# A softmax step queued behind the next head's shuffle, and weight halves made at other points, in a float32 transformer kernel on one core

## The chip, the cores and the metric

The kernel runs on one core of a Trainium2 chip. The metric is the device time of one execution in microseconds (us). TensorE is called PE below, VectorE DVE, ScalarE ACT, GpSimd POOL, and SyncE, which issues most DMAs, SP.

## The reference

Two blocks are computed for 256 tokens of width 1024 in float32. The first is two layers: a differential attention with 8 heads (this is where the main edit lies), a feed-forward, a short gated convolution, a feed-forward, each with a layer norm. The second is a parallel mixer, a cross attention to 256 memory tokens, and a product-key expert layer with 16384 experts, each with an RMS norm in front. Of the differential attention:

```
q, k: rotated on their first 16 of 64 dims; two score maps per head (c = 0, 1)
p = softmax(mask(q k / 8))                    # per map
a = p[0] - lam * p[1]
o = rms_norm(a @ v, g_sub) * (1 - lam_init)
out = o @ w_o
```

## The kernel before

**Weights.** Every product is made of three matmuls with a high and a low part of each operand (`mm3`, L329 to L331). `Stream` loads the weights in units of 1 MB by SP into two `raw` buffers, in the order of use. A unit has two halves. `pre(n)` makes the high parts of all halves below n on ACT (L231, tile `wh`); `split(n)` makes the low parts (L243, tile `wl`, `raw - wh`) on the engine that `W.sub` names for the half: V is DVE, G is POOL. When both halves of a unit are split, its `raw` buffer is free and the next load is issued. Order is manual: every engine runs its instructions in the order in which the program emits them.

**Attention.** A loop over 13 steps `st` is a pipeline over the 8 heads h. In step st: PE projects q and k of head st (`qk_proj`, ACT copies them out, L660), transposes the weights `at` of head st-3 (`pv_a`) and the output of head st-5 (`o_T`, low part on DVE, L749), multiplies by v for head st-4 (`pv_b`; ACT squares, L732; DVE rs2a, L325; POOL the inverse root, L320). `qk_rot` rotates head st: a shuffle on DVE (L666), then three products and sums on POOL (L668, L670, L672), which PE's scores wait for. `scores` of head st-1: PE (L683), DVE the maxima (L685 to L687), ACT the exponentials (L689, L696). `pv_n` scales on DVE (L739). `W.split` makes two low halves on DVE for the head after next. `soft` (L703 to L708) turns the exponentials of a head into `at`: six DVE instructions, a reciprocal, a product with lambda, and twice a scaling and a fused product and sum. From step 8 on there is no rotation, and PE multiplies by `wo0` and projects memory keys (`mem_k0`, `mem_k1`) between the heads.

**Boundaries.** `finish` ends a layer: last matmuls for token halves t = 0 and 1 (`last_mm`), residual and norm (`fa`, `fb`), transposes on PE (`to_T`), with a piece of memory projection (`mem_v`, `mem_k`) on PE as cover. `finish_two` is the one in front of the mixer, where a layer norm and an RMS norm follow each other; the one with `early=2` is the mixer's output boundary. `lam` makes lambda from 256 numbers.

Of the kernel before, what the change touches and what calls it, by code (L numbers as in the profile page):

```python
# [263 lines left out]
def body(ctx, tc, I, O):  # L264
    nc = tc.nc
    V, A, P, G = nc.vector, nc.scalar, nc.tensor, nc.gpsimd
# [136 lines left out]
    LNS = {}  # L403
# [36 lines left out]
    def rms_b(src, key, gb):  # L440
        ss = LNS.pop(key)
        a = sm([128, 2], name="ssa")
        V.tensor_scalar(a[:, 0:1], ss[:, 0:1], 1.0 / D, 1e-6, op0=OP.mult, op1=OP.add)
        V.scalar_tensor_tensor(a[:, 1:2], ss[:, 1:2], 1.0 / D, a[:, 0:1], op0=OP.mult, op1=OP.add)
        rs = inv_sqrt_pool(a[:, 1:2], 1, "rs1")
        if "hg" in LNS:
            r = LNS.pop("hg")
            V.tensor_scalar(r[:, 0:512], r[:, 0:512], rs, None, op0=OP.mult)
            A.activation(r[:, 512:], r[:, 512:], AF.Copy, scale=rs)
            return r  # L450
        r = wp.tile([128, D], F32, name="r")
        for s in (slice(0, 512), slice(512, 1024)):
            V.scalar_tensor_tensor(r[:, s], src[:, s], rs, gb[:, s], op0=OP.mult, op1=OP.mult)
        return r
# [10 lines left out]
    def last_mm(acc, items, t, nb, part=None):  # L465
        n = len(items)
        a, b = (0, n) if part is None else (0, n // 2) if part == 0 else (n // 2, n)
        for i in range(a, b):
            x, kt, w, j = items[i]
            wj = w(j)  # L470
            c = nb * 512
            mm3(acc[t][nb], x[0][:, kt, t * 128:t * 128 + 128], x[1][:, kt, t * 128:t * 128 + 128],
                wj[0][:, c:c + 512], wj[1][:, c:c + 512], False, i == n - 1)

    def finish_two(acc, items, fa, fb, x, fa0, fb0):
        last_mm(acc, items, 1, 0)
        last_mm(acc, items, 1, 1)
        W.sub = [V, V]
        W.pre(2 * W.i + 3)
        r0 = fb(0)  # L480
        fa(1, 0)
        fa(1, 1)
        W.split(2 * W.i + 3)
        W.sub = [G, G]
        W.look = 0
        for g in fa0:
            g()
        r1 = fb(1)
        W.split(2 * W.i + 2)
        src0 = r0()  # L490
        src1 = r1()
        for g in fb0:
            g()
        T0 = to_T(src0, 0, x, True)
        T0()
        W.split(2 * W.i + 1)
        to_T(src1, 1, x)
        W.split(2 * W.i + 2)
        W.look = 2
        W.sub = [V, V]  # L500
# [5 lines left out]
    def finish_any(acc, items, fa, fb, x, fa0=(), fb0=(), two=False, early=0, first=2, warm=0):  # L506
        if fb0 and not two:
            W.sub = [V, G]
        for nb in range(2):
            last_mm(acc, items, 0, nb, 0)  # L510
        for nb in range(2):
            last_mm(acc, items, 0, nb, 1)
            if nb == 0:
                W.sub = [G, G]
                W.split(2 * W.i + first)
            fa(0, nb)
        if two:
            return finish_two(acc, items, fa, fb, x, fa0, fb0)
        src0 = fb(0)
        last_mm(acc, items, 1, 0)  # L520
        if early:
            W.sub = [V, V]
            last_mm(acc, items, 1, 1)
            W.pre(2 * W.i + first + early)
        if early == 2:
            W.split(2 * W.i + first + 1)
        fa(1, 0)
        if early == 2:
            W.split(2 * W.i + first + 2)
        if not early:  # L530
            last_mm(acc, items, 1, 1)
        fa(1, 1)
        if callable(src0):
            src0 = src0()
        W.look = 0
        for f in fa0:
            f()
        W.look = 2
        T0 = to_T(src0, 0, x, True)
        if warm:  # L540
            ps = bank()
            xf = items[0][0][0].rearrange("p a b -> p (a b)")
            for i in range(warm):
                P.matmul(ps, xf[:, 0:128], xf[:, 0:512], start=True, stop=True)
        src1 = fb(1)
        if callable(src1):
            src1 = src1()
        T0()
        if early != 1:
            W.split(2 * W.i + 2)  # L550
        for f in fb0:
            f()
        to_T(src1, 1, x)
        W.sub = [V, V]
# [77 lines left out]
    for nb in range(2):  # L632
        pss = [bank(), bank()]
        for hf in range(2):
            w = W.get(("v0", nb * 2 + hf))
            proj_mov(pss, w, xT, hf * 4)
            if (nb, hf) == (1, 0):
                mem_norm(0)
                lam()
        for t in range(2):  # L640
            A.activation(v0[:, t, nb * 512:nb * 512 + 512], pss[t], AF.Copy)

# [8 lines left out]
    def abank(name, ok):  # L651
        return accp.tile([128, 512], F32, name=name) if ok else bank()
# [88 lines left out]

    def o_T(h):
        on = ON.pop(h)
        ps = abank("acc01", h < 3)
        for t in range(2):
            ts = slice(t * 128, t * 128 + 128)
            P.transpose(ps[:, ts], on[:, ts], ident)
        A.activation(oT[0][:, h, :], ps[:, :256], AF.Copy, scale=gs)
        V.scalar_tensor_tensor(oT[1][:, h, :], ps[:, :256], gs, oT[0][:, h, :].bitcast(F32), op0=OP.mult,  # L749
                               op1=OP.subtract)  # L750
# [38 lines left out]
    for st in range(8 + 5):  # L789
        W.look = 0 if 0 < st < 9 else 2  # L790
        if st < 8:
            qk_proj(st)
        if st in (1, 2):
            low = to_T(mem_in[st - 1], st - 1, mT, True)
        if st == 8:
            acc = acc_banks()
        if st in (8, 9):
            w_o(acc, oT, "wo0", st - 8)
        if st == 10:
            mem_k0(0)  # L800
        if st == 11:
            mem_k1(0)
        if st == 12:
            w_o(acc, oT, "wo0", 2, js=(0,))
        if 0 <= st - 3 < 8:
            pv_a(st - 3)
        if 0 <= st - 5 < 8:
            o_T(st - 5)
        if st == 12:
            w_o(acc, oT, "wo0", 2, js=(1,))  # L810
            W.split(2 * W.i + 4)
        if 0 <= st - 4 < 8:
            pv_b(st - 4)
        if st < 8:
            qk_rot(st)
        if st in (1, 2):
            low()
        if st == 0:
            W.split(2 * W.i + 3)
        if 0 <= st - 1 < 8:  # L820
            W.pre(2 * W.i + 4)
            if st == 1:
                W.split(2 * W.i + 2)
            scores(st - 1)
            if 0 <= st - 4 < 8:
                pv_n(st - 4)
            W.split(2 * W.i + 4)
        elif 0 <= st - 4 < 8:
            pv_n(st - 4)
        if 0 <= st - 1 < 8:  # L830
            soft(st - 1)

    def ln_boundary(acc, items, h, gi, fa0, fb0, early=0):
        hn = hp.tile([128, 2, D], F32, name="h")
# [895 lines left out]
```

## Time and profile before

| | |
|---|---|
| median of 3 runs | 1673.63 us (1673.27 to 1678.7) |
| the profiled execution | 1675.48 us |
| its span, first to last instruction | 1673.2 us |
| mean granted PE clock | 0.997 of full speed |
| busy: PE, DVE, ACT, POOL | 1642.3, 1168.1, 818.4, 442.5 us |

Times in the rows are us from the span's start. The profiled execution's own time is 2.3 us more than its span and 1.85 us more than the median. A busy time is an average over stages that are bounded by different engines, so it has to be read stage by stage.

### The profile page before, as it was taken

How to read it: one execution, taken by the hardware profiler on the slowest of the kernel's cores; microseconds unless marked ns; L12 is line 12 of the kernel's file. 1: busy time of each engine (PE TensorE's matmuls, PEld its weight loads, DVE VectorE, ACT ScalarE, POOL GpSimd, SP SyncE). 2: the span in 40 equal slices, each digit the busy share in tenths (PEclk: the TensorE clock that was granted, in tenths of full speed). 3: DMA queues.
4: the chain of work that ended last, by engine and by line, in shares of the span. 5: the costliest groups of instructions: out<-in, count | busy, mean ns of one | idle time of the engine just before them, and what ended most of it. 6: DMA issues, size and time to landing. Idle time of an engine off the chain costs nothing.

```text
span 1673.2 us, 27599 instructions
## 1 busy us (share of the span) xinstructions
PE 1642.3 (98%) x11024; PEld 1496.0 (89%) x11024; DVE 1168.1 (70%) x2076; ACT 818.4 (49%) x1268; POOL 442.5 (26%) x434
## 2 busy tenths in 40 slices
PE   8999999999999998999999999999999999999997
PEld 7989999899999986987989999999999888888886
DVE  5987554666655456776458898889898666666665
ACT  5664444444444445765454555444443544444444
POOL 0532000110300002001015788788611211111111
PEclk9999999999999999999999999999999999999999
DMA  8446777555555563534355666666544656566664
GB/s 286 154 144 238 246 243 239 176 202 200 199 194 178 201 227 138 179 104 168 112 195 152 191 188 180 192 184 181 149 151 140 213 202 222 203 220 203 219 203 176
DMA packets 80416, 317.48 MB, mean 190 GB/s; under 512 B 25120, under 2 KB 41760, under 8 KB 45344
## 3 DMA queue, kind: packets, MB, share of 16 engines
q1 hardware_dynamic: 59120, 304.38, 53.0%
q0 software_dynamic: 20736, 10.56, 4.2%
q8 instruction: 86, 1.41, 0.3%
q10 hardware_dynamic: 432, 0.79, 0.1%
q14 instruction: 42, 0.34, 0.1%
HBM read 303.04 MB, written 10.55 MB: 187 GB/s over the span
## 4 chain that ended last, share of the span: by engine, by line
PE 57%; DVE 2%; ACT 1%; DMA 1%; issue 1%; POOL 0%; POOLq 0%; ACTq 0%; SPq 0%; DVEq 0%
PE mm L329 10%; PE mm L331 10%; PE mm L330 10%; PE acc L330 8%; PE acc L329 7%; PE acc L331 7%; PE acc L1600 2%; DVE wl L243 1%; DMA big<-in_subk_dram 0%; PE mm L1479 0%; PE mm L1355 0%; PE mm L1322 0%; DMA raw<-in_ws_dram 0%; DMA raw<-in_vec_dram 0%; POOL rs L320 0%
## 5 line engine op out<-in xcount | busy, mean ns | idle before, releaser
L243 DVE TENSOR_TENSOR wl<-raw,wh 128x1024 fp32r<-128x1024 f32 (+1 forms) x525 | 644.8, 1247 | 249.8 <-ACT wh L231 248.6
L231 ACT ACTIVATE wh<-raw 128x1024 fp32r<-128x1024 f32 (+1 forms) x537 | 553.8, 1055 | 375.7 <-PE acc L331 180.0
L329 PE MATMUL mm<-xTh,wh 128*128 128x256 f32 x2328 | 659.5, 283 | 0.0
L331 PE MATMUL mm<-xTh,wl 128*128 128x256 f32 x2328 | 654.9, 281 | 2.0 <-DVE wl L243 2.0
L330 PE MATMUL mm<-xTl,wh 128*128 128x256 f32 x2328 | 654.3, 281 | 0.0
L329 PEld LDWEIGHTS mm<-xTh,wh 128*128 128x128 f32 x2328 | 440.8, 189 | 3.8 <-issue 1.0
L331 PEld LDWEIGHTS mm<-xTh,wl 128*128 128x128 f32 x2328 | 440.6, 189 | 3.1 <-DVE wl L243 3.1
L330 PEld LDWEIGHTS mm<-xTl,wh 128*128 128x128 f32 x2328 | 440.8, 189 | 0.8
L1511 POOL DMA_INDIRECT gd<-slots,idx x128 | 252.3, 1971 | 84.7 <-issue 32.0
L330 PE MATMUL acc<-wl,xTh 128*128 128x512 f32 x632 | 251.4, 398 | 0.6 <-DVE wl L243 0.6
L329 PE MATMUL acc<-wh,xTh 128*128 128x512 f32 x632 | 250.1, 396 | 1.7 <-DVE xTl L749 1.4
L331 PE MATMUL acc<-wh,xTh 128*128 128x512 f32 x504 | 197.6, 392 | 0.0
L329 PEld LDWEIGHTS acc<-wh,xTh 128*128 128x128 f32 x632 | 118.6, 188 | 32.3 <-DVE xTl L749 1.9
L330 PEld LDWEIGHTS acc<-wl,xTh 128*128 128x128 f32 x632 | 118.7, 188 | 28.5 <-DVE wl L243 1.9
L1558 POOL TENSOR_TENSOR big<-big,oj 128x256 f32<-128x256 f32 x64 | 57.6, 899 | 289.1 <-DMA oj<-gd 289.1
L243 POOL TENSOR_TENSOR wl<-raw,wh 128x1024 fp32r<-128x1024 f32 x12 | 29.0, 2425 | 324.7 <-ACT wh L231 324.7
L331 PEld LDWEIGHTS acc<-wh,xTh 128*128 128x128 f32 x504 | 94.6, 188 | 22.6
L895 DVE TENSOR_TENSOR sil<-sil,mm 128x256 f32<-128x256 f32 x44 | 18.5, 421 | 104.0 <-ACT sil L894 104.0
L894 ACT ACTIVATE sil<-mm 128x256 f32<-128x256 f32 x44 | 16.9, 385 | 148.6 <-PE mm L331 148.6
L362 DVE TENSOR_TENSOR xTh<-big,xTh 128x256 fp32r<-128x256 f32 x126 | 83.2, 660 | 0.0
L1510 POOL MEMSET spacer<- 1x1 f32 x128 | 78.5, 613 | 0.0
L330 PE MATMUL acc<-wl,hTh 128*128 128x512 f32 x176 | 69.6, 395 | 0.0
(391 smaller groups left out, 1814.1 us busy)
## 6 DMA issues: line engine op xcount, KB each, us to landing
raw<-in_ws_dram SPq DMA_DIRECT2D x131, 1024.0 KB, 5.1
raw<-in_us_dram SPq DMA_DIRECT2D x64, 1024.0 KB, 4.9
raw<-in_vs_dram SPq DMA_DIRECT2D x64, 1024.0 KB, 4.9
gd<-zt SPq DMA_DIRECT2D x32, 256.0 KB, 6.5
raw<-in_pq_dram SPq DMA_DIRECT2D x8, 1024.0 KB, 4.8
oj<-gd SPq DMA_DIRECT2D x64, 128.0 KB, 4.8
gb<-in_vec_dram POOLq DMA_DIRECT2D x12, 512.0 KB
gd<-slots,idx POOLq DMA_INDIRECT x128
```

Source lines behind the costliest of these rows:

```text
L231: self.nc.scalar.activation(h[:, s], self.R[i][:, k * HW:(k + 1) * HW][:, s], AF.Copy)
L243: self.sub[k].tensor_tensor(l[:, s], self.R[i][:, k * HW:(k + 1) * HW][:, s], h.bitcast(F32)[:, s], op=OP.subtract)
L329: P.matmul(ps, lh, rh, start=first, stop=False)
L330: P.matmul(ps, lh, rl, start=False, stop=False)
L331: P.matmul(ps, ll, rh, start=False, stop=last)
L362: V.tensor_tensor(l, src, h.bitcast(F32), op=OP.subtract)
L894: A.activation(s, pg[:, :256], AF.Silu)
L895: V.tensor_tensor(s, s, pg[:, 256:], op=OP.mult)
L1510: G.memset(spacer, 0.0)
L1511: d = G.indirect_dma_start(out=gd, out_offset=bass.IndirectOffsetOnAxis(ap=idx[:, h, k:k + 1], axis=0), in_=gate[:, 0, h, k:k + 1], in_off ...
L1558: G.tensor_tensor(b, b, GT.pop(c), op=OP.mult)
L1600: P.matmul(ps[:, i * 128:i * 128 + 128], oi[:, i, :], oj[:, i, :], start=True, stop=True)
```

## The change

- In the attention loop `soft(st - 1)` at a step's end becomes `soft(st - 2)` right behind `qk_rot(st)`: each head's softmax is emitted one step later, behind the next shuffle and ahead of the maxima.
- `lam()` moves from the value projection into step 0 of that loop.
- `o_T` of head 2 takes a rotating PSUM bank in place of the accumulator bank acc01.
- In front of the mixer, the third half of the two `mem_v` units is split on POOL ahead of the norm's work and the fourth on DVE; before, the third was on DVE behind the norm's first part and the fourth on POOL.
- At the mixer's output boundary, two low halves move from between the norm's instructions to behind them. `rms_b` gets a condition that this order needs.

```diff
@@ rms_b
-        if "hg" in LNS:
+        if key[1] == 1 and "hg" in LNS:
@@ finish_two
-        W.sub = [V, V]
-        W.pre(2 * W.i + 3)
+        W.sub = [G, V]
+        W.split(2 * W.i + 3)
+        W.pre(2 * W.i + 4)
         r0 = fb(0)
         fa(1, 0)
         fa(1, 1)
-        W.split(2 * W.i + 3)
+        W.split(2 * W.i + 4)
@@ finish_any
-        src0 = fb(0)
         last_mm(acc, items, 1, 0)
         if early:
             W.sub = [V, V]
             last_mm(acc, items, 1, 1)
+        if early == 2:
+            fa(1, 0)
+        src0 = fb(0)
+        if early:
             W.pre(2 * W.i + first + early)
-        if early == 2:
-            W.split(2 * W.i + first + 1)
-        fa(1, 0)
-        if early == 2:
-            W.split(2 * W.i + first + 2)
+        if early != 2:
+            fa(1, 0)
...
+        if early:
+            W.split(2 * W.i + 1)
         T0()
-        if early != 1:
+        if not early:
             W.split(2 * W.i + 2)
@@ the value projection
                 mem_norm(0)
-                lam()
@@ o_T
-        ps = abank("acc01", h < 3)
+        ps = abank("acc01", h < 2)
@@ the attention loop
             qk_rot(st)
+        if 0 <= st - 2 < 8:
+            soft(st - 2)
...
             W.split(2 * W.i + 3)
+            lam()
...
-        if 0 <= st - 1 < 8:
-            soft(st - 1)
```

In the attention loop, DVE's queue of one step before, from the two low weight halves of a step through the softmax to the next step's first maxima (`acc_953` is a score bank):

```order
L243 TENSOR_TENSOR wl<-raw,wh 128x1024 x2
L703 RECIPROCAL rc<-su 128x4
L704 TENSOR_TENSOR rc<-rc,nlam 128x2
L707 TENSOR_SCALAR pe<-pe,rc 128x128
L708 SCALAR_TENSOR_TENSOR at<-pe,rc 128x128
L707 TENSOR_SCALAR pe<-pe,rc 128x256
L708 SCALAR_TENSOR_TENSOR at<-pe,rc 128x256
L749 SCALAR_TENSOR_TENSOR xTl_339<-acc_924,gs,xTh_338 128x256
L325 TENSOR_SCALAR rs2a<-oss 128x2
L666 STREAM_SHUFFLE qksw<-qkraw 128x512
L685 MEMSET acc_953 64x2x64
```

The same stretch of the changed kernel, whose lines from the attention on are 2 higher (L705 to L710 are the softmax, L668 is the shuffle):

```order
L243 TENSOR_TENSOR wl<-raw,wh 128x1024 x2
L751 SCALAR_TENSOR_TENSOR xTl_328<-acc_917,gs,xTh_327 128x256
L325 TENSOR_SCALAR rs2a<-oss 128x2
L668 STREAM_SHUFFLE qksw<-qkraw 128x512
L705 RECIPROCAL rc<-su 128x4
L706 TENSOR_TENSOR rc<-rc,nlam 128x2
L709 TENSOR_SCALAR pe<-pe,rc 128x128
L710 SCALAR_TENSOR_TENSOR at<-pe,rc 128x128
L709 TENSOR_SCALAR pe<-pe,rc 128x256
L710 SCALAR_TENSOR_TENSOR at<-pe,rc 128x256
L687 MEMSET acc_953 64x2x64
```

The softmax moved from ahead of the low part of `o_T`, rs2a and the shuffle to directly behind the shuffle; POOL's three rotation instructions, whose queue is unchanged, start when the shuffle ends.

In front of the mixer, POOL's queue before, from the copy of the memory's transposed tile (L978) on; `rs_6578` is the norm of t = 0, `rs_6623` that of t = 1:

```order
L978 DMA xTl_6504<-mTl 128x2048
L320 TENSOR_TENSOR rs_6578<-rs1a,nhalf 128x1
L426 TENSOR_TENSOR h<-r,gb 128x512 x2
L320 TENSOR_TENSOR rs_6623<-rs1a,nhalf 128x1
L243 TENSOR_TENSOR wl<-raw,wh 128x1024
```

And in the changed kernel:

```order
L981 DMA xTl_6504<-mTl 128x2048
L243 TENSOR_TENSOR wl<-raw,wh 128x1024
L320 TENSOR_TENSOR rs_6582<-rs1a,nhalf 128x1
L426 TENSOR_TENSOR h<-r,gb 128x512 x2
L320 TENSOR_TENSOR rs_6629<-rs1a,nhalf 128x1
```

POOL's weight half now stands ahead of the norm's inverse root instead of behind both.

At the mixer's output boundary, DVE's queue before (`acc_7877` and `acc_7878` are the accumulators of t = 0, `acc_7879` and `acc_7880` those of t = 1):

```order
L453 SCALAR_TENSOR_TENSOR r<-h,rs_8129,gb 128x512 x2
L243 TENSOR_TENSOR wl<-raw,wh 128x1024
L458 TENSOR_TENSOR h<-h,acc_7879 128x512
L463 TENSOR_TENSOR r<-h,gb 128x512
L243 TENSOR_TENSOR wl<-raw,wh 128x1024
L458 TENSOR_TENSOR h<-h,acc_7880 128x512
L463 TENSOR_TENSOR r<-h,gb 128x512
```

And in the changed kernel, where the residual of t = 1 begins ahead of the norm of t = 0:

```order
L458 TENSOR_TENSOR h<-h,acc_7879 128x512
L463 TENSOR_TENSOR r<-h,gb 128x512
L443 TENSOR_SCALAR ssa<-ssh 128x1
L444 SCALAR_TENSOR_TENSOR ssa<-ssh,ssa 128x1
L453 SCALAR_TENSOR_TENSOR r<-h,rs_8158,gb 128x512 x2
L458 TENSOR_TENSOR h<-h,acc_7880 128x512
L463 TENSOR_TENSOR r<-h,gb 128x512
L443 TENSOR_SCALAR ssa<-ssh 128x1
L444 SCALAR_TENSOR_TENSOR ssa<-ssh,ssa 128x1
L448 TENSOR_SCALAR r<-r,rs_8213 128x512
L243 TENSOR_TENSOR wl<-raw,wh 128x1024
```

The two halves no longer stand between the residual of t = 0 and that of t = 1; one follows the norm, the other the transposes' low parts.

## Rows read from the trace of the kernel before

**Rows 1.** The first part of the page: busy time, share of the span and instructions of each engine.

```profile
PE 1642.3 (98%) x11024; PEld 1496.0 (89%) x11024; DVE 1168.1 (70%) x2076; ACT 818.4 (49%) x1268; POOL 442.5 (26%) x434
```

**Rows 2.** Busy time of the engines (PE, PE's weight loads, DVE, ACT, POOL, each with its instructions) in two stretches of 20 us of the attention; the last three columns are PE's granted clock, DMA share and GB/s.

```profile
60.00:80.00 20.00, 18.92 (x157) 17.66 (x155) 19.39 (x46) 12.83 (x38) 10.19 (x8) 1.00 0.51 176
80.00:100.00 20.00, 17.10 (x128) 15.12 (x128) 19.42 (x49) 11.33 (x37) 13.03 (x11) 1.00 0.40 141
```

**Rows 3.** What PE waited for between 34 and 142 us: us in total, times, longest.

```profile
PE acc L683 <- POOL qk L672: 1.8, 3, 0.8
PE acc L329 <- DVE xTl L749: 1.4, 1, 1.4
...
PE mm L683 <- POOL qk L672: 0.7, 1, 0.7
```

**Rows 4.** The attention in order of time, DVE: shuffles of heads 2, 5, 6 and 7, and between those of 5 and 6 the instructions with which the parts of a step begin (three of the softmax); last, a pair of low halves with POOL idle. Start, duration, engine, line, operation.

```profile
53.74 0.76 DVE L666 STREAM_SHUFFLE qksw<-qkraw 128x512 f32<-128x512 f32 x1
...
79.67 0.75 DVE L666 STREAM_SHUFFLE qksw<-qkraw 128x512 f32<-128x512 f32 x1
80.43 0.17 DVE L685 MEMSET acc<- 64x128 f32 x1
82.52 3.82 DVE L243 TENSOR_TENSOR wl<-raw,wh 128x1024 fp32r<-128x1024 f32 x2
86.27 0.16 DVE L703 RECIPROCAL rc<-su 128x4 f32<-128x4 f32 x1
86.46 0.16 DVE L704 TENSOR_TENSOR rc<-rc,nlam 128x2 f32<-128x2 f32 x1
86.98 0.35 DVE L708 SCALAR_TENSOR_TENSOR at<-pe,rc 128x128 f32<-128x128 f32 x1
88.04 0.48 DVE L749 SCALAR_TENSOR_TENSOR xTl<-acc,gs,xTh 128x256 fp32r<-128x256 f32 x1
88.50 0.73 DVE L666 STREAM_SHUFFLE qksw<-qkraw 128x512 f32<-128x512 f32 x1
...
97.32 0.73 DVE L666 STREAM_SHUFFLE qksw<-qkraw 128x512 f32<-128x512 f32 x1
...
108.35 2.35 DVE L243 TENSOR_TENSOR wl<-raw,wh 128x1024 fp32r<-128x1024 f32 x2
```

**Rows 5.** The attention in order of time, POOL: the rotation of head 0, and that of head 5.

```profile
39.18 1.29 POOL L668 TENSOR_TENSOR qksw<-qksw,rope 128x512 f32<-128x512 f32 x1 [4.84 <-DVE qksw L666]
40.43 2.28 POOL L670 TENSOR_TENSOR qk<-qkraw,rope 128x512 f32<-128x512 f32 x1
...
80.50 1.29 POOL L668 TENSOR_TENSOR qksw<-qksw,rope 128x512 f32<-128x512 f32 x1
81.76 1.30 POOL L670 TENSOR_TENSOR qk<-qkraw,rope 128x512 f32<-128x512 f32 x1
83.13 2.13 POOL L672 TENSOR_TENSOR qk<-qk,qksw 128x512 f32<-128x512 f32 x1
```

**Rows 6.** DVE and POOL at once, elsewhere, in order of time: a weight half on DVE during the rotation of head 0; the norm's fused products on DVE during POOL's weight half in front of the mixer; a small DVE instruction during POOL's products L1137 in the mixer.

```profile
39.28 2.27 DVE L243 TENSOR_TENSOR wl<-raw,wh 128x1024 fp32r<-128x1024 f32 x1 [0.18 <-ACT wh L231]
...
632.30 2.50 POOL L243 TENSOR_TENSOR wl<-raw,wh 128x1024 fp32r<-128x1024 f32 x1
632.49 3.53 DVE L428 SCALAR_TENSOR_TENSOR h<-r,rs,gb 128x512 f32<-128x512 f32 x2
...
737.72 2.52 POOL L1137 TENSOR_TENSOR h<-h,gb 128x512 f32<-128x512 f32 x2 [52.97 <-ACT r L1136]
739.29 0.98 DVE L1139 TENSOR_SCALAR ss<-ss 128x8 f32<-128x8 f32 x1
```

**Rows 7.** The same attention step, ACT: the scaling of the maxima, with which the exponentials begin, and the end of the squares behind them.

```profile
82.12 0.21 ACT L689 ACTIVATE nb<-mx 128x4 f32<-128x4 f32 x1 [3.25 <-DVE mx L687]
...
85.57 0.26 ACT L732 ACTIVATION_READ_ACCUMULATOR on<-acc 128x1 f32 x1
```

**Rows 8.** PE in the attention: the scores of step 5, and the first matmul of step 11.

```profile
85.31 0.93 PE L683 MATMUL acc<-qk 64*128 64x128 f32 x8 [0.75 <-POOL qk L672]
...
115.43 0.36 PE L329 MATMUL mm<-mTh,wh 128*128 128x256 f32 x1
```

**Rows 9.** The value projection: PE's wait behind lambda.

```profile
31.88 0.39 PE L331 MATMUL mm<-xTh,wl 128*128 128x256 f32 x1 [0.76 <-DVE wl L243]
```

**Rows 10.** In front of the mixer: the high part of the third half on ACT; PE's two waits for low halves, and its first transposes.

```profile
622.18 1.06 ACT L231 ACTIVATE wh<-raw 128x1024 fp32r<-128x1024 f32 x1 [1.26 <-DMA raw<-in_ws_dram]
...
631.00 0.50 PE L330 MATMUL mm<-wl,mTh 128*128 128x512 f32 x1 [2.43 <-DVE wl L243]
634.86 0.50 PE L330 MATMUL mm<-wl,mTh 128*128 128x512 f32 x1 [0.79 <-POOL wl L243]
637.82 1.32 PE L370 MATMUL mm<-cst,r 128*128 128x128 f32 x8
```

**Rows 11.** The mixer's output boundary: two low halves on DVE, PE's two waits in the transposes.

```profile
785.93 1.22 DVE L243 TENSOR_TENSOR wl<-raw,wh 128x1024 fp32r<-128x1024 f32 x1
788.39 1.22 DVE L243 TENSOR_TENSOR wl<-raw,wh 128x1024 fp32r<-128x1024 f32 x1
...
792.56 0.63 PE L370 MATMUL mm<-cst,r 128*128 128x128 f32 x4 [2.46 <-ACT xTh L373]
793.63 1.11 PE L370 MATMUL mm<-cst,r 128*128 128x128 f32 x4 [0.44 <-ACT r L449]
```

## The prediction

> **What bounds the kernel now.** The busy times come first: PE works 98% of the span [rows 1], so about 31 us is all that can be won, and only a stretch in which PE stands idle can give any of it. The stretches of the attention come next: between 60 and 100 us PE lacks 1.08 and 2.90 us, while DVE is busy 19.4 of 20 us in both [rows 2]. That is the sign of another bound: in these steps DVE sets the pace and PE waits. What PE waits for there is the rotated head (L672 on POOL, 1.8 and 0.7 us) and the release of an accumulator bank (1.4 us) [rows 3].
>
> So I read DVE's queue in order of time. From the shuffle of head 5 to that of head 6 it takes 8.83 us without a gap [rows 4]: shuffle 0.76, maxima and the scaling behind them 2.09 (80.43 to 82.52), two low halves 3.75, softmax 1.77 (86.27 to 88.04), the low part of `o_T` with rs2a 0.46. PE's own work in a step is this less its wait of 0.75 [rows 8], 8.1 us. The low halves take 3.82 here and 2.35 at 108.35, where POOL is idle [rows 4]: 1.47 us of the step is lost while POOL rotates.
>
> **How DVE and POOL lock each other.** The rotation of head 0 shows it. A low half is issued 0.10 us after L668 and takes 2.27 us [rows 6] where half a pair takes 1.2: it stands until L668 ends (40.45) and then runs 1.1, to 41.55. L670, next on POOL, takes 2.28 instead of 1.30: it stands until the low half ends and then runs [rows 5]. So one instruction at a time goes through, and the two engines take turns. The softmax's own kinds are held too: two fused products took 3.53 us, to 636.02, since POOL's half ran to 634.80, and a TENSOR_SCALAR on 128x8, however small, took 0.98, to the end of L1137 at 740.24 [rows 6]. The maxima in PSUM are not held: 1.69 us to the scaling on ACT (80.43 to 82.12) with POOL busy throughout [rows 4, 5, 7]. The Trainium skill ("SBUF — State Buffer", section "Who interferes with whom") says the same of DVE instructions with two SBUF inputs or in a 2-port mode: whoever issues first holds the shared ports for a whole instruction. It says nothing of turns. By it alone the softmax could lose as little as one rotation instruction (second rival); by the turns in the rows it loses three.
>
> **The softmax moved.** Before, it ran after POOL had finished: L672 ends at 85.26, the reciprocal starts at 86.27 [rows 4, 5]. Now it starts with the rotation. With S as the shuffle's start: the reciprocal is at S+0.76, the product with lambda at S+0.95; L668 starts at S+0.83 (79.67 to 80.50) and is first. It ends at S+2.1 (1.26 from start to start). Then the product slips through, L670 runs to S+3.4, the first scaling slips through, L672, with L668's 1.29 where it stands alone, runs to S+4.75. The first fused product and the rest need 1.06 more (86.98 to 88.04): the softmax ends at S+5.8 instead of S+2.53, 3.3 us later. The low halves, now past the rotation, give back 1.47. After the softmax DVE needs 2.09 + 2.28 + 0.46, which would bring the next shuffle at S+10.6. But rs2a, ahead of it, waits for ACT's squares, which follow the maxima and the exponentials: 1.69 + 3.71 (82.12 to 85.83 [rows 7]) brings S+11.2, and this is later. Before, the softmax hid that chain.
>
> Five such periods from the shuffle of head 2 to that of head 7 make 56.0 us against 43.6 before (53.74 to 97.32 [rows 4]): +12.4. The shuffle of head 2 itself comes some 1.2 earlier, because softmax 0 (1.77) no longer stands ahead of it, less about 0.6 that lambda costs in front of the shuffle of head 1. Behind the shuffle of head 7 the queue is S+11.2 for one more locked step, then softmax 6 (1.8), maxima (1.7), scaling and two halves (2.8), 0.5 and softmax 7 (1.8), and 1.2 of PE work to the first matmul of step 11: 21.0, against 18.1 before (97.32 to 115.43 [rows 4, 8]), +2.9. Together 12.4 - 1.2 + 2.9 = **+14**. This is an estimate by the turns above. Bounds of the lock's part: nothing lost to it gives the first rival; three turns a step, taken here, is all that three POOL instructions can take.
>
> **Lambda and the bank.** PE's wait of 0.76 behind lambda [rows 9] goes, but PE then reaches a stretch paced by DVE, so it counts 0 here (0.76 if DVE does not pace). The bank of head 2 takes away the wait of 1.43 [rows 3]; here DVE is late anyway and it counts 0. The rotating bank that it uses instead is wanted by the transposes of step 8, behind 5.6 us of `w_o` on PE (24 matmuls).
>
> **In front of the mixer.** PE waits 2.43 and 0.79 for low halves [rows 10]. The third half's high part is done at 623.24 [rows 10]; with 2.5 on POOL [rows 6] its low part is there at 625.8, and PE wants it at 628.6. The fourth falls on DVE at the place of the third, just in time: 3.2 us of waits go. The transposes behind them hang on the norm, which gains less: the 2.3 us that POOL's later half held the fused products [rows 6] (3.53 for a pair, of which 1.2 lie behind it) go away, some 0.3 of which the norm's inverse root takes up, and POOL's earlier half, ahead of the inverse root and beside DVE, costs some 0.5. I take **-1.5**, with 0 and -3.2 as bounds.
>
> **The output boundary.** Two low halves, 1.22 each, leave the queue ahead of the norm of t = 1 [rows 11], and one part of 0.7 that waited behind them moves up. PE's second transposes wait 2.46 and 0.44, first for ACT and the norm. That norm comes 2.4 earlier, but ACT's copies of `mem_v`, which stand behind PE's own end, still hold the transposes: **-1.6**, bounds 0 and -2.9. The halves are wanted by the projection 4 us after the transposes, so their delay is covered.
>
> **Sum.** +14 - 1.5 - 1.6 = +10.9. On the profiled execution's 1675.5 this gives 1686.4; its 1.85 over the median taken off, 1673.6 + 10.9 = **1684.5 us**, 0.65% slower.
>
> **Rivals.**
> First, *the softmax is not held* (the end on the other side). If its small instructions slip past the rotation, a step needs 7.4 us on DVE (8.83 - 1.47) and 2.53 + 1.69 + 3.71 = 7.9 along ACT, both under PE's 8.1. Then PE's waits of 1.8, 0.7 and 1.4 go [rows 3], and 0.76 [rows 9]: -4.7. With both boundaries 1673.6 - 7.8 = **1665.8**. For it: no row has a softmax beside a rotation. Against it: every row with a two-input instruction on DVE beside a product on POOL. It decides from a step under 8.1 us on.
> Second, *one turn only*: POOL loses its turn after L668 and the softmax runs through (86.46 to 88.04, 1.58) to S+3.7. The step is 3.7 + 1.69 + 3.71 = 9.1, five are 45.5 (+1.9), head 2 starts 1.2 earlier, the tail adds 0.8: +1.5, less 3.1: **1672.0**, no measurable change.
> Third, within the slow case, *the boundaries give nothing*: POOL's half in front of the root costs what PE's waits bring. Then 1687.6. The rows for it are the 0.5 us above; against it, both waits of PE are for these halves.
>
> **Chances and range.** The held softmax 0.60 (1680 to 1688: the attention 3 us less if a turn is lost here and there, the boundaries between their bounds), one turn 0.13, not held 0.27. What can be told from no change is 0.3%, 5.0 us: slower 0.57 (of the held case a little falls inside), same 0.17, faster 0.26. The forecast is 1684.5; a range for 8 in 10 must reach over all three cases, from 1665.0, just below the first rival, to 1687.5.
>
> **What the new profile would show.** In the attention: shuffles some 11 us apart (8.1 in the first rival, 9.1 in the second), products and scalings of the softmax of 0.5 to 1.3 us in place of 0.16 to 0.48, low halves of 1.2, PE idle about 3 us a step. In front of the mixer: no wait for low halves, transposes 1.5 us earlier after the last matmul of the feed-forward. At the output boundary: no low half between the norm's parts, and a wait of about 1 in place of 2.46. Wrong it would be if the softmax's instructions keep their durations beside L668 to L672, or if shuffles come on ACT's copy without a backlog on DVE.

## The result, and the profile after

The changed kernel takes **1682.93 us** (median of four runs, 1680.3 to 1688.3), the kernel before beside it 1673.66: a ratio of 1.0056, with a 95% interval from 1.0040 to 1.0072. It is 9.4 us slower (6.7 to 12.0), where 10.9 were forecast. Its profiled execution took 1680.9 us with a span of 1679.1, so it lies 2.0 below its median, and that of before 1.85 above. The two traces therefore differ by only 5.9 us in span, and part of what follows asks where the other microseconds sit.

PE's busy time has hardly changed; in the first part of the page of after (the same row as [rows 1]):

```profile
PE 1646.7 (98%) x11024; PEld 1499.7 (89%) x11024; DVE 1176.0 (70%) x2076; ACT 819.3 (49%) x1268; POOL 439.4 (26%) x434
```

The stretches of the attention have (the columns of [rows 2]: PE, PEld, DVE, ACT, POOL, PE's granted clock, DMA share, GB/s), and so have PE's waits in them (as [rows 3]):

```profile
60.00:80.00 20.00, 17.49 (x124) 15.75 (x124) 18.06 (x34) 9.88 (x30) 8.37 (x7) 0.91 0.43 158
80.00:100.00 20.00, 17.19 (x118) 15.07 (x119) 18.65 (x35) 11.12 (x36) 9.05 (x8) 0.91 0.31 106
```
```profile
PE acc L685 <- ACT pe L698: 3.6, 1, 3.6
PE acc L749 <- DVE on L741: 3.1, 2, 1.6
PE mm L749 <- DVE on L741: 2.4, 2, 1.8
PE mm L685 <- ACT qkraw L662: 1.1, 1, 1.1
```

PE no longer waits for POOL's rotated head at all. It waits for what stands behind the maxima: the exponentials (L698), the scaled outputs (L741) and the copied head, which follows the exponentials on ACT (L662): 10.2 us in these four rows. DVE still has little room, and PE's clock is now below full in both stretches. PE lacks 2.51 and 2.81 us of 20 in them, some 1.5 us a step where the prediction's sign was "about 3": a part of the waiting shows as longer matmuls instead (the eight scores at 93.02 take 2.01 us, in [rows 8] 0.93). The same step as in [rows 4, 5], head 5, on DVE and then POOL; the last line of each is from the step of head 7, and the row on ACT is the end of the squares ahead of the shuffle at 95.19:

```profile
84.22 0.75 DVE L668 STREAM_SHUFFLE qksw<-qkraw 128x512 f32<-128x512 f32 x1
...
85.06 0.16 DVE L706 TENSOR_TENSOR rc<-rc,nlam 128x2 f32<-128x2 f32 x1
85.25 1.22 DVE L709 TENSOR_SCALAR pe<-pe,rc 128x128 f32<-128x128 f32 x1
86.51 1.28 DVE L710 SCALAR_TENSOR_TENSOR at<-pe,rc 128x128 f32<-128x128 f32 x1
87.70 1.44 DVE L709 TENSOR_SCALAR pe<-pe,rc 128x256 f32<-128x256 f32 x1
89.18 0.48 DVE L710 SCALAR_TENSOR_TENSOR at<-pe,rc 128x256 f32<-128x256 f32 x1
...
91.78 2.35 DVE L243 TENSOR_TENSOR wl<-raw,wh 128x1024 fp32r<-128x1024 f32 x2
94.60 0.48 DVE L751 SCALAR_TENSOR_TENSOR xTl<-acc,gs,xTh 128x256 fp32r<-128x256 f32 x1 [0.47 <-ACT xTh L750]
95.11 0.17 DVE L325 TENSOR_SCALAR rs2a<-oss 128x2 f32<-128x2 f32 x1
95.19 0.73 DVE L668 STREAM_SHUFFLE qksw<-qkraw 128x512 f32<-128x512 f32 x1
...
106.99 1.31 DVE L706 TENSOR_TENSOR rc<-rc,nlam 128x2 f32<-128x2 f32 x1
```
```profile
84.38 0.71 POOL L320 TENSOR_TENSOR rs<-rs2a,nhalf 128x2 f32<-128x2 f32 x1 [6.37 <-DVE rs2a L325]
85.06 1.33 POOL L670 TENSOR_TENSOR qksw<-qksw,rope 128x512 f32<-128x512 f32 x1
86.34 1.29 POOL L672 TENSOR_TENSOR qk<-qkraw,rope 128x512 f32<-128x512 f32 x1
87.71 1.29 POOL L674 TENSOR_TENSOR qk<-qk,qksw 128x512 f32<-128x512 f32 x1
...
106.98 1.30 POOL L670 TENSOR_TENSOR qksw<-qksw,rope 128x512 f32<-128x512 f32 x1
```
```profile
94.82 0.26 ACT L734 ACTIVATION_READ_ACCUMULATOR on<-acc 128x1 f32 x1
```

Three instructions of the softmax that took 0.29 to 0.35 us at the step's end take 1.22, 1.28 and 1.44. Each ends 0.08 to 0.16 us behind the end of one POOL product (86.39, 87.63, 89.00), and POOL starts its next one in between without delay. The softmax ends 5.44 us behind the shuffle's start. The low halves take 2.35 instead of 3.82, and DVE then waits 0.47 for ACT, whose chain started late. The squares end at 95.08, and rs2a, ahead of the next shuffle, starts at 95.11. The step is 10.97 us instead of 8.83.

In front of the mixer, PE's transposes and the small projection behind them (the rows that answer to the end of [rows 10]), and the clock in the stretch before 649.05 and behind it:

```profile
646.60 1.32 PE L370 MATMUL mm<-cst,r 128*128 128x128 f32 x8 [1.16 <-DVE r L453]
649.17 1.75 PE L370 MATMUL mm<-cst,r 128*128 128x128 f32 x8 [1.25 <-DVE r L453]
650.57 2.06 PE L998 MATMUL mm<-xTh,wih 128*8 128x256 f32 x8
...
654.59 0.40 PE L329 MATMUL mm<-wh,xTh 128*128 128x512 f32 x1
```
```profile
645.05:649.05 4.00, 1.71 (x10) 0.84 (x8) 2.52 (x7) 3.33 (x7) 1.08 (x2) 1.00 0.25 107
649.05:652.45 3.40, 3.25 (x17) 2.17 (x18) 3.12 (x5) 2.54 (x4) 2.38 (x1) 0.59 0.00 0
```

Both waits of [rows 10] for low halves are gone. PE works through and then waits 1.16 and 1.25 us for the norms of the two halves. Behind these waits the clock falls to the lower of its two levels: the eight matmuls at 650.57 take 2.06 us, in the kernel before 1.29.

At the output boundary, two answers to [rows 11], and the same stretch's clock before (first two rows) and after:

```profile
799.05 1.47 PE L370 MATMUL mm<-cst,r 128*128 128x128 f32 x12
801.49 0.66 PE L370 MATMUL mm<-cst,r 128*128 128x128 f32 x4 [0.96 <-ACT r L449]
```
```profile
789.00:792.80 3.80, 1.34 (x11) 1.06 (x10) 2.89 (x7) 2.50 (x6) 1.19 (x2) 1.00 0.60 175
792.80:796.20 3.40, 2.96 (x16) 2.72 (x15) 2.39 (x4) 2.68 (x5) 0.00 (x0) 0.57 0.71 275
```
```profile
798.90:802.70 3.80, 2.84 (x24) 2.44 (x23) 3.46 (x5) 3.44 (x8) 0.56 (x1) 1.00 0.45 142
801.50:805.50 4.00, 4.00 (x33) 3.93 (x34) 3.55 (x5) 2.91 (x4) 0.00 (x0) 1.00 0.08 26
```

Waits of 2.46 and 0.44 have become one of 0.96. In addition the kernel before ran the stretch behind its waits at the lower level (0.57 is mostly 0.5), and the changed one does not.

### The profile page after: what moved, and what is told of

The parts are those of the page before. It is cut to its first block, busy times and chain, and to the rows that moved or that the text cites. A ratio compares the mean times of both kernels' runs of the same rounds, so it can differ in the third digit from the quotient of the medians.

```text
span 1679.1 us, 27604 instructions
## 1 busy us (share of the span) xinstructions
PE 1646.7 (98%) x11024; PEld 1499.7 (89%) x11024; DVE 1176.0 (70%) x2076; ACT 819.3 (49%) x1268; POOL 439.4 (26%) x434
## 3 DMA queue, kind: packets, MB, share of 16 engines
q8 instruction: 86, 1.41, 0.3%
## 4 chain that ended last, share of the span: by engine, by line
PE 59%; DVE 1%; ACT 1%; issue 1%; POOL 0%; POOLq 0%; DVEq 0%; ACTq 0%
PE mm L329 10%; PE mm L331 10%; PE mm L330 10%; PE acc L330 8%; PE acc L329 8%; PE acc L331 8%; PE acc L1603 2%; PE mm L1482 0%; PE mm L1358 0%; PE mm L1325 0%; PE mm L341 0%; PE mm L998 0%; DVE wl L243 0%; POOL rs L320 0%; PE mm L370 0%
## 5 line engine op out<-in xcount | busy, mean ns | idle before, releaser
L243 DVE TENSOR_TENSOR wl<-raw,wh 128x1024 fp32r<-128x1024 f32 (+1 forms) x525 | 636.0, 1231 | 245.0 <-ACT wh L231 243.6
```

Of the source, the lines that this page charges most:

```text
L243: self.sub[k].tensor_tensor(l[:, s], self.R[i][:, k * HW:(k + 1) * HW][:, s], h.bitcast(F32)[:, s], op=OP.subtract)
```

## Where the time went, by stage

From the rows of each trace on PE one can take four marks: the first transposes behind the attention (L370), the first matmul of the memory's last projection in front of the mixer, the first one of the mixer's own projections, and at the output boundary the first residual on DVE (L458) and the first scores behind it (L1322 in before). The table gives, for every kernel profiled here, the mean distance of the shuffles of heads 2 to 7, the end of the attention by the first mark, the front (second to third mark) and the output boundary (the last two), all in us, and the median time. The kernel before, run again beside each, took 1673.5 to 1673.8.

```
kernel      shuffles  attention ends  front           output boundary  median time
before      8.72      133.76          22.1            25.4 (low clock) 1673.7
after       10.88     146.31          20.5 (low clock) 22.0            1682.9
soft_only   11.04     149.13          21.4            25.0 (low clock) 1686.3
rest        8.72      133.47          19.3            22.0             1667.3
front_only  8.72      133.93          20.5 (low clock) 25.2 (low clock) 1673.0
out_only    8.72      133.68          21.3            22.0             1670.8
rot_less    9.95      140.83          20.5 (low clock) 22.0            1674.4
rot_more    12.07     154.49          20.4 (low clock) 22.0            1689.4
rot_dve     10.25     142.47          19.9            21.8             1677.3
soft_max    8.85      134.86          21.2 (low clock) 22.0            1671.5
lam_back    11.01     147.41          21.7 (low clock) 22.0             1683.2
bank_back   10.98     149.61          20.8 (low clock) 22.0             1684.6
rest_warm   8.71      133.54          21.6            21.8             1668.5
```

From before to after: the attention costs +12.55, the front gives -1.6, the output boundary -3.4; the feed-forward between attention and front is 1.05 shorter and the rest 0.7 shorter in this pair of executions, though no edit touches them. Together +5.9, the difference of the spans. In the other kernels that keep the old front it takes 21.3 and 21.4, and the feed-forward is 0.7 to 0.8 shorter than in before (soft_only, out_only), so some of both lies in the profiled execution of before and not in the change: there PE waited 2.43 us for the first low half, in these two 1.67 and 1.61. Over all thirteen traces the feed-forward takes 487.6 to 489.2 us, so its 1.05 lies within the scatter.

## The experiments

The first four take the change apart. The lines of the diffs are those of the kernel named in the expectation.

**soft_only**, the softmax alone:

```diff
         if st < 8:
             qk_rot(st)
+        if 0 <= st - 2 < 8:
+            soft(st - 2)
...
-        if 0 <= st - 1 < 8:
-            soft(st - 1)
```

> The kernel before with one edit: softmax of head st-2 directly behind the shuffle of head st, instead of softmax of head st-1 at the end of the step. Theory (DVE's softmax and POOL's rotation take turns, one instruction at a time): the shuffles stand some 10.9 us apart, three softmax instructions of a step take 1.2 to 1.45 us, and the time is 11 to 14 us above the kernel before. Rival (the loss of the whole change comes from the softmax together with the moved lambda and the bank of head 2): less than 8 us above. If the softmax is not what costs: within 3 us of the kernel before.

Measured: 1686.29 us, ratio 1.0078 (1.0064 to 1.0092), that is 13 us above the kernel before. The shuffles stand 11.04 us apart, and the softmax of head 3 reads, in DVE's order of time:

```profile
86.52 1.21 DVE L707 TENSOR_SCALAR pe<-pe,rc 128x128 f32<-128x128 f32 x1
87.76 1.28 DVE L708 SCALAR_TENSOR_TENSOR at<-pe,rc 128x128 f32<-128x128 f32 x1
88.96 1.45 DVE L707 TENSOR_SCALAR pe<-pe,rc 128x256 f32<-128x256 f32 x1
```

So the moved softmax alone accounts for the whole loss, and for more than the net.

**rest**, everything but the softmax:

```diff
-        if 0 <= st - 2 < 8:
-            soft(st - 2)
...
         elif 0 <= st - 4 < 8:
             pv_n(st - 4)
+        if 0 <= st - 1 < 8:
+            soft(st - 1)
```

> The changed kernel with the softmax alone put back to the end of the step (softmax of head st-1); lambda, the bank and both boundaries stay changed. Theory: the shuffles stand 8.8 us apart again, the low halves take 3.8 us a pair again; the boundaries give back 1.6 to 2.7 us in front of the mixer and 2.4 to 3.4 us at its output, the bank and lambda 0 to 2 us: 4 to 7 us below the kernel before. Rival (the boundaries gained only because the attention ended late): within 2 us of the kernel before.

Measured: 1667.31 us, ratio 0.9971 (0.9960 to 0.9983): this beats both kernels. The step is that of before again (DVE, head 5 to head 6; the low halves pay for the rotation, the softmax does not):

```profile
79.52 0.73 DVE L668 STREAM_SHUFFLE qksw<-qkraw 128x512 f32<-128x512 f32 x1
82.37 3.82 DVE L243 TENSOR_TENSOR wl<-raw,wh 128x1024 fp32r<-128x1024 f32 x2
...
86.51 0.29 DVE L709 TENSOR_SCALAR pe<-pe,rc 128x128 f32<-128x128 f32 x1
86.83 0.35 DVE L710 SCALAR_TENSOR_TENSOR at<-pe,rc 128x128 f32<-128x128 f32 x1
...
88.36 0.75 DVE L668 STREAM_SHUFFLE qksw<-qkraw 128x512 f32<-128x512 f32 x1
```

The attention ends 0.3 us earlier than in before, so lambda and the bank give next to nothing here, as the prediction had it. The gain lies at the two boundaries.

**front_only** and **out_only**, one boundary each (the hunks of `finish_two`, and of `finish_any` with the condition in `rms_b`, from the diff above, on the kernel before):

```diff
-        W.sub = [V, V]
-        W.pre(2 * W.i + 3)
+        W.sub = [G, V]
+        W.split(2 * W.i + 3)
+        W.pre(2 * W.i + 4)
...
```

> The kernel before with the edit in front of the mixer alone (third weight half of the boundary on POOL ahead of the norm, fourth on DVE). Theory: PE's waits of 2.43 and 0.79 for low halves go, a wait of 1.2 for the norm takes their place: 1.6 to 2.7 us below the kernel before. If the granted clock of PE falls behind that wait, as it did in the changed kernel, 1.1 of it are lost again. Rival (POOL's half in front of the inverse root costs what PE's waits bring): no change.

> The kernel before with the edit at the mixer's output boundary alone (residual of t = 1 ahead of the norm of t = 0, the two low halves behind it). Theory: PE's wait of 2.46 goes and the one behind the norm of t = 1 becomes about 1: 1.6 to 2.4 us below the kernel before, 3.4 if the granted clock stays up as it did in the changed kernel. Rival (the copies of the memory's values on ACT hold the transposes as before): no change.

Measured: front_only 1673.00 us, ratio 0.9995 (0.9986 to 1.0004), no change that can be told; out_only 1670.80 us, ratio 0.9986 (0.9977 to 0.9995), 2 to 3 us below. In the trace of front_only the waits for low halves are gone as in after, and the front is 0.8 us shorter than the 21.3 of out_only. It could be two: behind the waits for the norm the clock is at its lower level for the whole second stretch, in rest (second pair of rows) it is not:

```profile
632.50:636.50 4.00, 1.70 (x10) 0.84 (x8) 2.40 (x8) 3.30 (x9) 1.08 (x2) 1.00 0.32 133
636.50:639.90 3.40, 2.99 (x14) 2.16 (x15) 3.20 (x6) 2.36 (x4) 2.38 (x1) 0.50 0.00 0
```
```profile
632.07:636.07 4.00, 1.70 (x10) 0.86 (x9) 2.52 (x6) 3.33 (x7) 1.08 (x2) 1.00 0.21 88
636.07:639.47 3.40, 3.29 (x25) 2.17 (x26) 2.92 (x5) 2.99 (x5) 2.83 (x2) 1.00 0.00 0
```

The first stretch of front_only ends 0.41 us ahead of the second transposes, that of rest 0.01; where both end 0.12 ahead, PE was busy 1.41 and 1.81 us of the 4. The front takes 20.5 us in the first and 19.3 in the second. Of these 1.2, 0.4 is a longer wait for the norm (1.46 against 1.06), and 0.8 is the fall: from the second transposes to the mixer's own projections front_only takes 5.12 us and rest 4.30. In all five traces that keep their clock there this takes 4.29 or 4.30 us, in six others 5.0 to 5.4 and in lam_back 6.4, so that a fall costs 0.7 to 1.1 us, and once 2.1. By the table, the clock fell behind the front in seven of the nine traces with the new order and PE's waits left as they are, and in none of the three with the old order, although PE waited longer there in all. In the old order the long waits come earlier: PE was busy 2.73 to 2.75 of the 4 us ahead of the second transposes, in the new one 1.3 to 1.8. The output boundary takes 22.0 in out_only and 21.8 to 22.0 in every kernel with the new order, and 25.0 to 25.4 in every one with the old.

The next four are on the mechanism: the number of POOL's products beside the softmax, and the softmax's place.

**rot_less** and **rot_more**, one product fewer and one more:

```diff
-        G.tensor_tensor(qk, qk, sw, op=OP.add)
```
```diff
         G.tensor_tensor(qk, qk, sw, op=OP.add)
+        G.tensor_tensor(sw3, sw3, rope[:, None, 256:].to_broadcast([128, 2, 256]), op=OP.mult)
```

> The changed kernel with the third rotation product on POOL (the sum of the two rotated parts) left out: the scores are computed from the first part alone, so this part of the computation is missing. Theory (each product on POOL costs the softmax one turn): two instructions of a softmax of 1.2 to 1.4 us instead of three, shuffles 9.7 us apart instead of 10.97, 6 steps of it: 7 to 8 us below the changed kernel, some 1675. Rival (the softmax is late for another reason than POOL, the length of the step comes from ACT and PE): shuffles stay 11 us apart, 1682.

> The changed kernel with a fourth product of the same size on POOL behind the three of each rotation; nobody reads what it writes. Theory (turns): a fourth instruction of the softmax, the last fused product, is held until it ends, about 1.4 instead of 0.48 us; shuffles 11.9 us apart instead of 10.97, 5 to 6 us above the changed kernel, some 1688. Rival (POOL's products delay the softmax only once, when they begin, or not at all): shuffles stay 11 us apart, 1682.

Measured: 1674.42 us and 1689.39 us, against 1682.9 with three. A step is 9.92 us with two products (80.68 to 90.60), 10.97 with three and 11.95 with four (77.41 to 89.36). The last two instructions of the softmax, scaling and fused product on 128x256, with two products on POOL, and with four:

```profile
84.20 0.34 DVE L708 TENSOR_SCALAR pe<-pe,rc 128x256 f32<-128x256 f32 x1
84.57 0.48 DVE L709 SCALAR_TENSOR_TENSOR at<-pe,rc 128x256 f32<-128x256 f32 x1
```
```profile
80.90 1.44 DVE L710 TENSOR_SCALAR pe<-pe,rc 128x256 f32<-128x256 f32 x1
82.38 1.45 DVE L711 SCALAR_TENSOR_TENSOR at<-pe,rc 128x256 f32<-128x256 f32 x1
```

Two products hold two instructions, four hold four, and each adds some 1.0 us to the step: this is the clearest evidence for the turns.

**rot_dve**, the rotation on DVE:

```diff
-        G.tensor_tensor(sw3, sw3, rope[:, None, 256:].to_broadcast([128, 2, 256]), op=OP.mult)
+        V.tensor_tensor(sw3, sw3, rope[:, None, 256:].to_broadcast([128, 2, 256]), op=OP.mult)
...
-        G.tensor_tensor(qk, qk, sw, op=OP.add)
+        V.tensor_tensor(qk, qk, sw, op=OP.add)
```

> The changed kernel with the three rotation products on DVE instead of POOL, so that POOL has nothing to do beside the softmax. Three products of 0.69 us are added to DVE's queue ahead of the softmax. Theory (the lock): the softmax takes 1.8 us again (instructions of 0.16 to 0.49 us), it ends 4.6 us behind the shuffle's start instead of 5.46, shuffles 10.1 us apart, 4 to 6 us below the changed kernel, some 1678, although DVE has more work. Rival (what counts is DVE's own load in front of the maxima, not the lock): shuffles 12 to 13 us apart, above 1688.

Measured: 1677.32 us, some 5.6 below the changed kernel, although DVE now does all of the rotation. The order of DVE in a step:

```profile
85.36 0.69 DVE L674 TENSOR_TENSOR qk<-qk,qksw 128x512 f32<-128x512 f32 x1
...
86.37 0.28 DVE L709 TENSOR_SCALAR pe<-pe,rc 128x128 f32<-128x128 f32 x1
86.69 0.35 DVE L710 SCALAR_TENSOR_TENSOR at<-pe,rc 128x128 f32<-128x128 f32 x1
```

With POOL silent beside the softmax, the same instructions, behind the rotation as before, take 0.28 and 0.35. It is POOL that holds them, not the place in the queue.

**soft_max**, the softmax behind the maxima:

```diff
-        if 0 <= st - 2 < 8:
-            soft(st - 2)
...
             scores(st - 1)
+            if st >= 2:
+                soft(st - 2)
...
+        if st == 9:
+            soft(7)
```

> The changed kernel with the softmax of head st-2 put behind the maxima of the step (and ahead of the scaling of the outputs and the low halves), instead of directly behind the shuffle. Theory: the maxima, which POOL does not hold, no longer wait for the softmax, so ACT's chain is early again; the softmax meets the last two products of the rotation and loses two turns, the low halves lose none: a step is 9.2 us on DVE, shuffles 9.0 to 9.3 us apart; 1667 to 1671, at most 3 us from the kernel with the softmax at the end of the step. Rival (each softmax that stands after the shuffle, wherever, costs three turns and 3.3 us): shuffles 10 us apart or more, above 1675. If the softmax is held once only: 8.5 us apart, 1664 to 1666.

Measured: 1671.54 us, ratio 0.9986 (0.9977 to 0.9995), just above the range expected and 4 us above rest; of these, by the table, the attention accounts for 1.4 and the front, where in this trace PE waited longer for the norm and the clock fell, for 1.9. From head 4 on a step takes 9.17 us, and two instructions are held, the first of them a product on two columns:

```profile
80.06 0.85 DVE L706 TENSOR_TENSOR rc<-rc,nlam 128x2 f32<-128x2 f32 x1
80.95 1.40 DVE L709 TENSOR_SCALAR pe<-pe,rc 128x128 f32<-128x128 f32 x1
82.39 0.35 DVE L710 SCALAR_TENSOR_TENSOR at<-pe,rc 128x128 f32<-128x128 f32 x1
```

Here ACT's chain is early and no wait for it is left, so a softmax that meets one product fewer, behind the maxima, saves most of the loss. It still costs 0.34 us more per step than at the step's end, where it meets no product at all.

The last three are on what the table left over.

**lam_back** and **bank_back**:

```diff
             if (nb, hf) == (1, 0):
                 mem_norm(0)
+                lam()
...
             W.split(2 * W.i + 3)
-            lam()
```
```diff
-        ps = abank("acc01", h < 2)
+        ps = abank("acc01", h < 3)
```

> The changed kernel with lambda alone put back between the matmuls of the value projection. The kernel with the softmax alone moved spent 2.8 us more in the attention than the changed one, and of its two missing edits only lambda and the bank touch the attention. Theory (lambda's wait of PE and DVE stays in front of a stretch paced by DVE and is carried through): the shuffle of head 2 is 0.75 later, and the attention ends 0.75 to 1.5 us later: 1683.5 to 1684.5. Rival (the two edits count for nothing there, the 2.8 us came from stretches at the lower clock): no change, within 0.5 us of the changed kernel. Rival (all of it is lambda): 2.8 us above.

> The changed kernel with the accumulator bank of head 2 alone put back (the output transposes of head 2 use the accumulator bank again). Theory: with the softmax moved, no wait of PE for this bank shows before step 8, so nothing changes, within 0.5 us of the changed kernel. Rival (the wait of 1.4 us for the bank's release comes back in front of the output projection): 1.4 to 2 us above.

Measured: 1683.19 and 1684.63 us (1.0050 to 1.0075 and 1.0053 to 1.0079 of before; the changed kernel's interval is 1.0040 to 1.0072): neither can be told from the changed kernel. The shuffle of head 2 is 0.63 later in lam_back (52.37 against 51.74; 0.75 expected), but in bank_back, where lambda stands as in the changed kernel, it is at 52.20, so this is no sign of lambda. PE's wait of 1.4 us for the bank ([rows 3]), which bank_back could have brought back, is not in its trace. Where the attention ends varies more than either, from 146.3 to 149.6 over the four kernels in which three products hold the softmax. PE's granted clock there, in stretches of 10 us from 50 to 140, is below full in two of the changed kernel (0.83 each) and in four of each of the others, down to 0.66. What of the 2.8 us between soft_only and after belongs to the two edits and what to the clock stays open; the clock is the likelier, by these stretches.

**rest_warm**, PE kept busy in the two waits in front of the mixer:

```diff
+        ps = bank()
+        xf = items[0][0][0].rearrange("p a b -> p (a b)")
+        for i in range(4):
+            P.matmul(ps, xf[:, 0:128], xf[:, 0:512], start=True, stop=True)
         T0 = to_T(src0, 0, x, True)
+        ps = bank()
...
+        for i in range(4):
+            P.matmul(ps, xf[:, 0:128], xf[:, 0:512], start=True, stop=True)
         T0()
```

> The kernel with all edits but the moved softmax, with four matmuls of 128x512 whose result nobody reads put in each of PE's two waits of 1.1 and 1.25 us for the norms in front of the mixer (0.23 us each). Theory (PE's clock falls for some 3.4 us behind these two waits in most executions, though not in the profiled one of the kernel without the extra matmuls; with PE busy it stays up): the stretch from the first matmul of the memory's projection to the first one of the mixer takes 19.3 us and never 20.5, 0.5 to 1 us below the kernel without them in the median, some 1666.5. Rival (the clock falls all the same, or the extra matmuls come later than the norm and hold the transposes): 0 to 1 us above it.

Measured: 1668.48 us, 1.2 above rest, ratio 0.9970 (0.9958 to 0.9981); the two can't be told apart. The clock stays at 1.00 through this stretch, but the transposes pay for it:

```profile
639.55 0.63 PE L370 MATMUL mm<-cst,r 128*128 128x128 f32 x4 [0.25 <-DVE r L453]
640.73 0.66 PE L370 MATMUL mm<-cst,r 128*128 128x128 f32 x4 [0.54 <-DVE xTl L378]
```

The second four of them are released by a low part of the first (0.54), by the look of it because the extra matmuls took a bank, and the stretch from the memory's last matmul to the mixer's first takes 9.64 us, against 8.31 in rest and 9.54 in after. Another 0.8 of its 21.6 us is a wait for a low half further ahead, which rest does not have and whose cause was not followed. The filling gained nothing here that can be told; rest had kept its clock in its trace without it.

## Why the prediction was right, point by point

Of the three cases the held softmax, given 0.60, is what the rows show, step by step. That the time lies in the stated range says little, since that reached from 1665.0 to 1687.5 over all three.

**The lock.** Three instructions a step are held, as forecast. At heads 2 to 6 they are not the same three. The reciprocal starts 0.12 us earlier than reckoned, so the product with lambda starts together with the rotation (85.06 both) and is not held; the turns then fall to the scaling, the fused product and the second scaling, and the softmax ends 5.44 us behind the shuffle's start; 5.8 were forecast. At head 7 the product at 106.99 meets the rotation at 106.98 and is held for 1.31: there it is the three of the sum, and the softmax ends 5.68 behind the shuffle. What settles so near a tie stays open. The rule of the Trainium skill ("SBUF — State Buffer", section "Who interferes with whom") that the one who issued first holds the shared ports for a whole instruction agrees with the rows as far as their starts can be told apart (the second scaling at 87.70 and POOL's third product at 87.71 can't); that POOL's next product does not get ahead of a waiting DVE instruction, nor DVE's of POOL's, is what rot_less and rot_more add. By that rule alone the second rival stood open; steps of 10.88 us, where it had 9.1, leave nothing of it.

**The chain along ACT.** It binds as forecast: DVE has an idle gap of 0.47 us a step that before had none. It shows at the low part of `o_T`, one instruction ahead of rs2a, where it was looked for; the squares, which the sum had rs2a wait for, end at 95.08, just as rs2a could start. The sum's 1.69 + 3.71 from the softmax's end on is 1.72 + 3.70 here. The step is 10.97 instead of 11.2, five of them 54.4 us instead of 56.0: **+10.8** where +12.4 stood in the sum.

**Head 2 and the tail.** The shuffle of head 2 comes 2.0 us earlier (51.74 against 53.74), not 1.2: lambda, in its new place, costs the shuffle of head 1 nothing (43.88 against 44.10), though two of its instructions are held there by the rotation of head 0. The tail from the shuffle of head 7 to the first matmul of step 11 takes 21.7 us (106.15 to 127.88), 21.0 forecast. Together +12.45, against the **+14** of the sum.

**Lambda and the bank.** Zero each was forecast, and -0.3 together is what rest shows in the attention.

**In front of the mixer.** -1.5 was forecast, and the trace has -1.6, but the step was put wrongly. The waits that go give 2.0 to 2.8 (from 21.3 or 22.1 to 19.3 in rest), more than the step's sum; a wait for the norm that varies (1.06 to 1.87) and the clock's fall behind it (0.7 to 2.1 in seven traces of nine), which the step did not have, take part or all of that surplus back. Against the old front of the other kernels after gains 0.8, and front_only gained 0.5 in the median: in size that is nearer to the third rival. Its reason, that POOL's half in front of the root costs what it brings, is not what the rows show: the root starts 0.37 us behind the value that it needs, in the kernel before 0.09.

**The output boundary.** This term was mis-sized: -1.6 with a bound of -2.9 stood in the sum, and the trace has **-3.4** (25.4 to 22.0; -3.0 to -3.2 against the other kernels with the old order). The waits are as forecast, 0.96 for "about 1". What is missing in the sum is the clock. It stood in the rows: in [rows 11] four transposes take 1.11 us at 793.63, while four of the same shape take 0.63 at 792.56. With 2.9 us of waits gone down to 0.96, 1.9 of the 3.4 are waits, and the other 1.5 is put down to the clock by difference; soft_only against the changed kernel gives the same 1.5.

**The sum.** By this pair of traces the terms are +12.5 - 1.6 - 3.4 = +7.5; against the other kernels with the old boundaries +12.5 - 0.8 - 3.1 = +8.6; the medians have +9.3, and the single edits by their medians +12.8 - 0.5 - 2.7 = +9.6. The forecast of +10.9 lies 1.6 above the difference of the medians. Both misses that can be named, 1.5 too much loss for the attention and 1.5 too little gain for the output boundary, point the same way, and together they are 3 us; that the time still fell within 1.6 is in part luck. The attention's end, which the other kernels with a softmax held by three products put up to 3 us later than after's profiled execution, may have made up the rest; no run shows it for the other executions of the changed kernel.

## What to carry to other kernels

Where two engines go through a shared resource in turns, count instructions, not microseconds: here each of POOL's products of 1.29 us cost one DVE instruction 0.7 to 1.2 us, however small that one was, so a chain of small dependent instructions is a poor thing to put beside a few long ones. Whether a few long ones would lose less at the same place was not tried. Before something is moved forward in a queue, look at what starts there at the same moment on the other engines, and which chain had been hidden behind it at its old place. In rows of matmuls read the duration as well as the wait: a group that takes nearly twice what its like takes (1.11 against 0.63) can show a fallen clock, and whoever removes the wait ahead of it may get both back, as at the output boundary. In front of the mixer the new order brought a fall that the old one did not have.

## What the runs showed that was not expected

A product on 128x2 took 0.85 us beside POOL (80.06 in soft_max) and 0.16 without it, while POOL's products kept their 1.29 us throughout: the small ones fit between two of them, and the whole price is paid on DVE. Beside weight halves of 1.2 us POOL had paid too (2.13 and 2.28 in [rows 5]).

PE's granted clock went to its lower level behind the waits of the old output boundary in all three kernels that have it (before, soft_only, front_only: PE busy 1.35 us in before, 1.48 and 1.49 in the others, of the 3.8 ahead of the first transposes with a wait), and in none of the ten with the new one (2.84 of the 3.8 ahead of its one wait's end in after, out_only and rest). In front of the mixer it was the other way round: never behind the old order's waits of 1.6 to 2.4, 0.8 and 1.25 us, in seven traces of nine behind the new order's two, of 1.1 to 1.9 and of 1.25. PE was busy 1.71 us of the 4 ahead in after, 1.41 in front_only and 1.31 in soft_max, where the clock fell, and 1.81 in rest and 1.31 in rot_dve, where it did not. So neither the sum of a stretch's waits nor PE's busy time ahead tells alone whether the clock falls. What decides there stays open, and with it how much of the changed kernel's wider scatter (8 us over four runs) is the clock.
